# Sums of weight blocks: from the vector engine to accumulating DMAs of GpSimd's queue

## The chip, the cores and the metric

The kernel runs on one core of one Trainium2 chip. The metric is the device time of one execution in microseconds, and a lower time is better. Five engines have instruction queues of their own and work each through its own queue in order: TensorE (PE in the profile; PEld is its weight load), VectorE (DVE), ScalarE (ACT), GpSimd (POOL) and SyncE (SP). An instruction that waits holds up all that stands behind it on its engine.

## The reference

The reference is a trunk of two layers on 512 tokens of width 1024 in float32. Each layer mixes (attention, a short convolution and an RWKV recurrence side by side, with one input and one output projection), and then has an MLP, which is all that matters here:

```python
for l in range(DEPTH):                       # DEPTH = 2
    ...                                      # mixing, x = x + mixed @ w_out[l]
    h = rms_norm(x, norm_mlp_g[l])
    x = x + jnp.square(jax.nn.relu(h @ w_mlp_up[l])) @ w_mlp_down[l]
return rms_norm(x, final_norm_g)
```

`w_mlp_up` is 1024 x 4096 and `w_mlp_down` 4096 x 1024.

## The kernel before

Every float32 product is made of three passes of TensorE. A weight block (128 x 512 elements, 256 KB) is loaded, ScalarE casts it to a high part (`act.copy`), and a subtraction makes the low part; high by high, high by low and low by high are added up in PSUM. The moving operand is split the same way.

The up projection of a layer has 32 groups of 128 columns. The first eight (`up`) are done plainly. The other 24 go in 12 pairs per layer, 24 pairs in all: `two(i0, i1)` computes the groups `i0` and `i1` together by seven products instead of eight, a scheme of the Strassen-Winograd kind. Each group's weight is two blocks (`w11`, `w12` of `i0`; `w21`, `w22` of `i1`), and the sequence is cut in two halves of 256. The seven products, in TensorE's order, are p1 (`w11`), p5, p6, p2 (`w12`), p7, p3 and p4 (`w22`); p5, p6, p7 and p3 have sums of blocks as weights. One product is 12 matmuls of 128 x 256. The sums stand in tiles `s1` to `s4`, made by VectorE in `sum_` (line 1461). `both` (lines 1455 and 1456) splits a block or a sum: the cast on ScalarE writes `shi_…`, the subtraction on VectorE writes `slo_…`. This is done a pair ahead: the blocks of pair n+1 are split while pair n is multiplied. `blocks` makes the combinations of the moving operand, `th`, once per layer.

`square` takes the two outputs of a pair: VectorE applies relu and a scale (`r`, line 1400), ScalarE squares (`m`, line 1402), then `kept` splits the result into `mh` (ScalarE) and `ml` (GpSimd, line 1392). These are the moving operands of the down projection.

After nearly every pair comes `down(h, js)`: four `dn` tiles, each 12 matmuls of 128 x 512 into PSUM tag `mm`, which has two buffers. VectorE adds each tile to the residual `x` (line 1516), which frees its buffer. So a `dn` tile can't start before the tile two ahead of it has been added. The down weights come through `weights` (lines 339, 344 and 345: load by SyncE, cast `whi` by ScalarE, subtraction `wlo` by VectorE), in a ring of three sets and a fourth spare one: the cast for a tile of the next `down` is made when a `dn` tile of this one has freed a set. In layer 1, no `down` stands between the last two pairs; what is left goes to `last_group` at the end (`dnF`).

In the MLP the order of each engine's queue is set when the program is built, by a scheduler of the language's tile layer; in the mixing part it is written out by hand. A tile's semaphores follow from the program order of its readers and writers.

Of the kernel before, what the change touches and what calls it, by code (L numbers as in the profile page):

```python
# [10 lines left out]
F32 = mybir.dt.float32  # L11
F32R = mybir.dt.float32r
# [4 lines left out]
ALU = mybir.AluOpType  # L17
# [6 lines left out]
P = 128  # L24
# [244 lines left out]
def tile_trunk(ctx: ExitStack, tc: tile.TileContext, xT, wts, prm_d, cst_d, lora_d, gup_d, lam_d, fin_d, out):  # L269
    nc = tc.nc  # L270
    act, dve, pool = nc.scalar, nc.vector, nc.gpsimd
# [195 lines left out]
    def last_group(fp, wbase, mids):  # L467
# [21 lines left out]

        eps = cp.tile([P, 12], F32, tag="lsum", name="epsF")[:, :1]  # L490
        dve.memset(eps, EPS)
        eye = fp.tile([P, 4, P], F32R, tag="s1", name="eyeF")[:, 0]
        act.copy(eye, ident)

        def norm(half, sq):
            q = slice(half * H, (half + 1) * H)
            pt = psum("rp", 4, f"pssF{half}")
            for i, a in enumerate((acc[:, q], sq)):
                for b in range(2):

                    pe.matmul(pt[:, b:b + 1], a[:, b * P:(b + 1) * P], ones1, start=(i == 0 and b == 0), stop=True,
                              skip_group_check=True)
            yy, xt = [cp.tile([P, n], F32, tag=k, bufs=b, name=f"{k}F{half}") for k, b, n in (("rr", 2, NB), ("rsx", 3, 48))]
            yy, xx, t = yy[:, :2], xt[:, :2], xt[:, 24:26]
            hi, lo = [fp.tile([P, 4, P], F32R, tag=k, name=f"r{p}F{half}")[:, 0, :2] for p, k in (("hi", "s2"), ("lo", "s3"))]
            act.activation(t, pt[:, :2], AF.Sqrt, bias=eps, scale=1.0 / D)
            dve.tensor_scalar(xx, pt[:, :2], 1.0 / D, EPS, ALU.mult, ALU.add)
            dve.reciprocal(yy, t)
            act.copy(hi, yy)
            dve.tensor_tensor(t, yy, yy, ALU.mult)  # L510
            dve.scalar_tensor_tensor(t, t, -0.5, xx, ALU.mult, ALU.mult)
            dve.scalar_tensor_tensor(t, t, 1.5, yy, ALU.add, ALU.mult)
            dve.tensor_tensor(lo, t, hi.bitcast(F32), ALU.subtract)
            yield

            rb = [psum("rp", 4, f"prbF{half}_{i}") for i in range(1 + half)]
            for i, r in enumerate((hi, lo)):
                for p in rb:
                    for b in range(2):
                        pe.matmul(p[:, b * P:(b + 1) * P], r[:, b:b + 1].to_broadcast([P, P]), eye, start=(i == 0 and b == 0),  # L520
                                  stop=(i == 1), skip_group_check=True)
            rbs = fp.tile([P, H], F32, tag="c0", bufs=2, name=f"rbs{half}")
            act.copy(rbs, rb[-1][:, :H])
            os_ = []
            for j in range(NK):
                o = fp.tile([P, H], F32, tag=("p1", "p5", "u2", "c1")[j // 2], bufs=2, name=f"o{half}_{j}")
                if j in ((2, 5) if half else (2, 5, 6, 7)):
                    pool.tensor_tensor(o, x[j][:, q], rbs, ALU.mult)
                else:
# [39 lines left out]
    for l in range(L):  # L569
# [807 lines left out]
        with ExitStack() as mx:  # L1377
# [14 lines left out]
                pool.tensor_tensor(lo, m, hi.bitcast(F32), ALU.subtract)  # L1392
                mids.append((hi, lo))

            def square(cs, name):

                r = fp.tile([P, S], F32, tag="r", bufs=2, name=f"r{name}")
                for i, c in enumerate(cs):
                    q = slice(i * H, i * H + c.shape[1])
                    dve.scalar_tensor_tensor(r[:, q], c, 0.0, rs[:, q], ALU.max, ALU.mult)  # L1400
                m = fp.tile([P, S], F32, tag="m", bufs=3, name=f"m{name}")
                act.activation(m, r, AF.Square)
                kept(m)
# [25 lines left out]

            def blocks(k):  # L1430
                b1, b2 = bn[k], bn[k + 4]
                t = [fp.tile([P, 2, H], F32, tag=f"s{2 * (k % 2) + i + 1}", name=f"t{l}_{k}_{i}") for i in range(2)]
                dve.tensor_tensor(t[0][:, 0], b1[:, 1], b1[:, 0], ALU.subtract)
                dve.tensor_tensor(t[0][:, 1], b2[:, 1], t[0][:, 0], ALU.subtract)
                dve.tensor_tensor(t[1][:, 0], b2[:, 1], b1[:, 1], ALU.subtract)
                dve.tensor_tensor(t[1][:, 1], b2[:, 0], t[0][:, 1], ALU.subtract)
                hi, lo = th[k] = [fp.tile([P, 4, H], F32R, tag=f"t{p}{k}", name=f"t{p}{l}_{k}") for p in ("hi", "lo")]
                for i in range(2):
                    u = slice(2 * i, 2 * i + 2)
                    act.copy(hi[:, u], t[i])  # L1440
                    dve.tensor_tensor(lo[:, u], t[i], hi[:, u].bitcast(F32), ALU.subtract)

            def two(i0, i1):

                n = f"{l}_{i0}"
                wg = wbase + NG_IN + NG_OUT

                def raw(i, a):
                    t = fp.tile([P, 4, P], F32, tag="sraw", bufs=6, name=f"raw{n}_{i}_{a}")
                    nc.sync.dma_start(t.rearrange("p k c -> p (k c)"), wts[wg + i, :, a * P:(a + 4) * P])  # L1450
                    return t

                def both(src, name):
                    hi, lo = [fp.tile([P, 4, P], F32R, tag=f"s{p}", bufs=5, name=f"s{p}{n}_{name}") for p in ("hi", "lo")]
                    act.copy(hi, src)  # L1455
                    dve.tensor_tensor(lo, src, hi.bitcast(F32), ALU.subtract)  # L1456
                    return hi, lo

                def sum_(name, a, b, op):
                    t = fp.tile([P, 4, P], F32, tag=name, name=f"{name}{n}")  # L1460
                    dve.tensor_tensor(t, a, b, op)
                    return t

                def small(name):
                    return fp.tile([P, H], F32, tag=name, bufs=2, name=f"{name}{n}")

                def product(pt, w, moving, first=True):

                    whi, wlo = w
                    for k in range(4):  # L1470
                        ahi, alo = moving(k)
                        pe.matmul(pt, whi[:, k], ahi, start=(first and k == 0), stop=False, skip_group_check=True)
                        pe.matmul(pt, whi[:, k], alo, start=False, stop=False, skip_group_check=True)
                        pe.matmul(pt, wlo[:, k], ahi, start=False, stop=(k == 3), skip_group_check=True)

                blk = lambda d, q: lambda k: [p[:, q * H:(q + 1) * H] for p in acts[4 * d + k]]
                smm = lambda q: lambda k: [p[:, q] for p in th[k]]
                pa, pb = [psum("rp", 4, f"p{i}{n}")[:, :H] for i in "ab"]
                pc = psum("at", 2, f"pc{n}")[:, :H]
                c0 = fp.tile([P, S], F32, tag="c0", bufs=2, name=f"c0{n}")  # L1480
                w11 = raw(i0, 0)
                product(pa, both(w11, "p1"), blk(0, 0))
                p1 = small("p1")
                act.copy(p1, pa)
                w21 = raw(i1, 0)
                w22 = raw(i1, 4)
                s1 = sum_("s1", w21, w22, ALU.add)
                product(pb, both(s1, "p5"), smm(0))
                p5 = small("p5")
                dve.tensor_copy(p5, pb)  # L1490
                s2 = sum_("s2", s1, w11, ALU.subtract)
                product(pa, both(s2, "p6"), smm(1), False)
                u2 = small("u2")
                act.copy(u2, pa)
                w12 = raw(i0, 4)
                product(pc, both(w12, "p2"), blk(1, 0))
                dve.tensor_tensor(c0[:, :H], pc, p1, ALU.add)
                s3 = sum_("s3", w11, w21, ALU.subtract)
                product(pa, both(s3, "p7"), smm(2), False)
                c1 = small("c1")  # L1500
                act.copy(c1, pa)
                dve.tensor_tensor(c1, c1, p5, ALU.add)
                s4 = sum_("s4", w12, s2, ALU.subtract)
                product(pb, both(s4, "p3"), blk(1, 1), False)
                dve.tensor_tensor(c0[:, H:], pb, u2, ALU.add)
                square([c0], f"{n}_0")
                product(pa, both(w22, "p4"), smm(3), False)
                square([pa, c1], f"{n}_1")

            def down(h, js):  # L1510

# [96 lines left out]
```

## Time and profile before

| | us |
|---|---|
| runs, device time | 1241.35, 1242.42, 1243.07 |
| median | 1242.42 |
| profiled execution, span from first to last instruction | 1241.5 |
| TensorE busy | 1230.0 |
| VectorE busy | 912.1 |
| ScalarE busy | 675.0 |
| GpSimd busy | 368.0 |

The profiled execution is listed by its span; no device time of its own stands beside it, so the span is compared with the median of the runs, 0.9 us above it. The granted clock of TensorE is 0.998. The DMA queues moved 127.90 MB, 103 GB/s on average, nearly all of it on SyncE's queue. In the profile's rows, `out<-in` are the program's tile names without their numbers, `xN` is a count, and the brackets at the end of a row of the timeline give the idle time of the engine just before and what ended it. Rows "start us, us, engine line operation" come from the chain of waits or the timeline. MATMUL rows overlap each other, so their single durations don't add up to TensorE's time.

### The profile page before, as it was taken

To read this page: it belongs to the slowest core of one execution; us is meant where nothing else is said; L and a number is where in the kernel's file an instruction comes from. 1 tells how busy PE (TensorE), PEld (TensorE's weight loads), DVE (VectorE), ACT (ScalarE), POOL (GpSimd) and SP (SyncE) were. 2 spreads that over 40 slices of the span, in tenths; PEclk is the share of its full clock that TensorE was granted. 3 is DMA by queue.
4 is the path that set the end of the run, shared out by engine and by line. 5 is a ranking of instruction groups with operands and counts; after the bars stand their busy time and mean duration, and the time that the engine had idled before them with its cause. 6 is when DMAs were issued, how large, how long until landed. Compare 5 with 4: busy or idle time off the path is not lost.

```text
span 1241.5 us, 24974 instructions
## 1 busy us (share of the span) xinstructions
PE 1230.0 (99%) x9492; PEld 1055.0 (85%) x9492; DVE 912.1 (73%) x1776; ACT 675.0 (54%) x1410; POOL 368.0 (30%) x457
## 2 busy tenths in 40 slices
PE   9999999999999999999999999999999999999997
PEld 6888888888899998989887888888888999998987
DVE  6787888868767676765766777887687767676753
ACT  6785655548445454544464657464583445454542
POOL 1263637342311111111026355464231211111111
PEclk9999999999999999999999999999999999999999
DMA  6523324142433333321235244332433333333121
GB/s 216 163 87 99 105 96 111 53 153 85 136 102 98 107 94 106 99 85 44 69 106 164 79 118 119 89 83 73 158 102 120 102 102 98 107 94 107 55 68 68
DMA packets 84695, 127.90 MB, mean 103 GB/s; under 512 B 21472, under 2 KB 25568, under 8 KB 84576
## 3 DMA queue, kind: packets, MB, share of 16 engines
q1 hardware_dynamic: 83568, 125.64, 33.1%
q8 instruction: 74, 1.21, 0.4%
q10 hardware_dynamic: 1008, 0.68, 0.2%
q14 instruction: 45, 0.37, 0.1%
HBM read 117.11 MB, written 9.18 MB: 102 GB/s over the span
## 4 chain that ended last, share of the span: by engine, by line
PE 93%; ACT 2%; DVE 2%; DMA 1%; POOL 1%; issue 1%; ACTq 0%; POOLq 0%; DVEq 0%
PE dn L282 25%; PE pj L282 20%; PE pa L282 11%; PE po L282 8%; PE up L282 7%; PE pb L282 6%; PE dnF L282 4%; PE pc L282 3%; PE sc L282 1%; DMA raw<-wts 1%; PE ptt L287 1%; PE pg L282 1%; PE pyy L282 1%; PE pzw L282 1%; PE pst L282 1%
## 5 line engine op out<-in xcount | busy, mean ns | idle before, releaser
L1392 POOL TENSOR_TENSOR ml<-m,mh 128x512 fp32r<-128x512 f32 x64 | 108.9, 1716 | 481.0 <-ACT mh L1391 340.6
L344 ACT CAST whi<-raw 128x512 fp32r<-128x512 f32 x142 | 87.4, 619 | 162.4 <-PE dn L282 152.8
L282 PE MATMUL dn<-mh,whi 128*128 128x512 f32 x448 | 174.8, 390 | 0.1
L282 PE MATMUL dn<-ml,whi 128*128 128x512 f32 x448 | 174.6, 390 | 0.0
L282 PE MATMUL dn<-mh,wlo 128*128 128x512 f32 x448 | 174.5, 390 | 0.0
L683 POOL TENSOR_TENSOR wlo<-raw,whi 128x512 fp32r<-128x512 f32 x84 | 111.0, 1321 | 213.1 <-ACT whi L671 175.4
L282 PE MATMUL pj<-ahim,whi 128*128 128x512 f32 x392 | 156.7, 400 | 0.4 <-DVE vf L1278 0.4
L282 PE MATMUL pj<-ahim,wlo 128*128 128x512 f32 x392 | 156.4, 399 | 0.0
L282 PE MATMUL pj<-alom,whi 128*128 128x512 f32 x392 | 155.9, 398 | 0.0
L1516 DVE TENSOR_TENSOR x<-dn,x 128x512 f32<-128x512 f32 x112 | 77.3, 690 | 103.1 <-PE dn L282 103.1
L671 ACT CAST whi<-raw 128x512 fp32r<-128x512 f32 x142 | 87.6, 617 | 83.3 <-PE pj L282 25.1
L345 DVE TENSOR_TENSOR wlo<-raw,whi 128x512 fp32r<-128x512 f32 x142 | 115.0, 811 | 11.2 <-ACT whi L344 8.3
L282 PEld LDWEIGHTS dn<-mh,wlo 128*128 128x128 f32 x448 | 84.1, 188 | 17.8
L282 PEld LDWEIGHTS dn<-mh,whi 128*128 128x128 f32 x448 | 84.1, 188 | 17.5 <-issue 0.4
L282 PEld LDWEIGHTS dn<-ml,whi 128*128 128x128 f32 x448 | 84.1, 188 | 16.7
L1455 ACT CAST shi_p<-s 128x512 fp32r<-128x512 f32 x96 | 59.6, 621 | 70.1 <-PE pa L282 55.1
L282 PEld LDWEIGHTS pj<-ahim,whi 128*128 128x128 f32 x392 | 73.9, 188 | 14.1 <-issue 0.8
L282 PEld LDWEIGHTS pj<-alom,whi 128*128 128x128 f32 x392 | 73.9, 188 | 13.9 <-issue 0.5
L282 PEld LDWEIGHTS pj<-ahim,wlo 128*128 128x128 f32 x392 | 73.9, 188 | 13.8 <-issue 0.2
L1456 DVE TENSOR_TENSOR slo_p<-s,shi_p 128x512 fp32r<-128x512 f32 x96 | 67.9, 708 | 19.7 <-ACT shi_p L1455 17.2
L282 PE MATMUL pa<-tlo,shi_p 128*128 128x256 f32 x288 | 81.3, 282 | 0.0
L282 PE MATMUL pa<-thi,shi_p 128*128 128x256 f32 x288 | 81.2, 282 | 0.0
(414 smaller groups left out, 3208.1 us busy)
## 6 DMA issues: line engine op xcount, KB each, us to landing
raw<-wts SPq DMA_DIRECT2D x389, 256.0 KB, 2.7
qs<-dqhi SPq DMA_DIRECT2D x24, 128.0 KB, 3.7
ks<-dkhi SPq DMA_DIRECT2D x24, 128.0 KB, 3.7
x<-xT SPq DMA_DIRECT2D x8, 256.0 KB, 4.6
dqhi<-qhi SPq DMA_DIRECT2D x6, 256.0 KB, 3.4
dqlo<-qlo SPq DMA_DIRECT2D x6, 256.0 KB, 3.4
dkhi<-khi SPq DMA_DIRECT2D x6, 256.0 KB, 2.7
dklo<-klo SPq DMA_DIRECT2D x6, 256.0 KB, 3.5
```

Source lines behind the costliest of these rows:

```text
L282: ins = nc.tensor.matmul(*a, **k)
L287: ins = nc.tensor.transpose(*a, **k)
L344: act.copy(hi[:, :n], raw[:, :n])
L345: (pool if a and lean[0] else dve).tensor_tensor(lo[:, :n], raw[:, :n], hi[:, :n].bitcast(F32), ALU.subtract)
L671: yield act.copy(hi[:, k0:k1], raw[:, k0:k1])
L683: yield eng.tensor_tensor(lo[:, k0:k1], raw[:, k0:k1], hi[:, k0:k1].bitcast(F32), ALU.subtract)
L1392: pool.tensor_tensor(lo, m, hi.bitcast(F32), ALU.subtract)
L1455: act.copy(hi, src)
L1456: dve.tensor_tensor(lo, src, hi.bitcast(F32), ALU.subtract)
L1516: dve.tensor_tensor(x[j], pt, x[j], ALU.add)
```

## The change

`sum_` goes. `begun` has SyncE load the first block of a sum straight into the sum's tile, and `plus` adds a further block to it by a DMA of GpSimd's queue with `accum_op=ALU.add`. Such a transfer can only add. So a pair's second output is computed with its sign turned: then every block enters with a plus, `square` takes the minimum with zero in place of the maximum before it squares, and `blocks` turns signs to match. The sums for p5, p6 and p3 are now one running sum in one tile (`w21`, then `+ w22`, `+ w11`, `+ w12`), and p7's is a second one (`w11 + w21`). Each tag has two buffers. A further block can only be added when both halves of the split have read the sum before it. Per pair: four sums of VectorE are gone, four accumulating DMAs of GpSimd are new, and nine blocks are loaded instead of four. The last group's small tiles take the same tags.

```diff
-                t = [fp.tile([P, 2, H], F32, tag=f"s{2 * (k % 2) + i + 1}", name=f"t{l}_{k}_{i}") for i in range(2)]
-                dve.tensor_tensor(t[0][:, 0], b1[:, 1], b1[:, 0], ALU.subtract)
-                dve.tensor_tensor(t[0][:, 1], b2[:, 1], t[0][:, 0], ALU.subtract)
+                t = [fp.tile([P, 2, H], F32, tag=("s1", "s3")[i], bufs=2, name=f"t{l}_{k}_{i}") for i in range(2)]
+                dve.tensor_tensor(t[0][:, 0], b1[:, 0], b1[:, 1], ALU.subtract)
+                dve.scalar_tensor_tensor(t[0][:, 1], t[0][:, 0], -1.0, b2[:, 1], ALU.mult, ALU.subtract)
                 dve.tensor_tensor(t[1][:, 0], b2[:, 1], b1[:, 1], ALU.subtract)
-                dve.tensor_tensor(t[1][:, 1], b2[:, 0], t[0][:, 1], ALU.subtract)
+                dve.scalar_tensor_tensor(t[1][:, 1], t[0][:, 1], -1.0, b2[:, 0], ALU.mult, ALU.subtract)
...
-                def sum_(name, a, b, op):
-                    t = fp.tile([P, 4, P], F32, tag=name, name=f"{name}{n}")
-                    dve.tensor_tensor(t, a, b, op)
+                def begun(tag, i, a):
+                    t = fp.tile([P, 4, P], F32, tag=tag, bufs=2, name=f"{tag}{n}")
+                    nc.sync.dma_start(t.rearrange("p k c -> p (k c)"), wts[wg + i, :, a * P:(a + 4) * P])
+                    return t
+                def plus(t, i, a):
+                    pool.dma_start(t.rearrange("p k c -> p (k c)"), wts[wg + i, :, a * P:(a + 4) * P], accum_op=ALU.add)
                     return t
...
-                w21 = raw(i1, 0)
                 w22 = raw(i1, 4)
-                s1 = sum_("s1", w21, w22, ALU.add)
-                product(pb, both(s1, "p5"), smm(0))
+                sm = plus(begun("s1", i1, 0), i1, 4)
+                product(pb, both(sm, "p5"), smm(0))
...
-                s2 = sum_("s2", s1, w11, ALU.subtract)
-                product(pa, both(s2, "p6"), smm(1), False)
+                product(pa, both(plus(sm, i0, 0), "p6"), smm(1), False)
...
-                s3 = sum_("s3", w11, w21, ALU.subtract)
-                product(pa, both(s3, "p7"), smm(2), False)
+                product(pa, both(plus(begun("s3", i0, 0), i1, 0), "p7"), smm(2), False)
...
-                s4 = sum_("s4", w12, s2, ALU.subtract)
-                product(pb, both(s4, "p3"), blk(1, 1), False)
+                product(pb, both(plus(sm, i0, 4), "p3"), blk(1, 1), False)
...
-                square([pa, c1], f"{n}_1")
+                square([pa, c1], f"{n}_1", ALU.min)
```

TensorE's order is the same in both programs. That of the other engines is not. ScalarE's queue in layer 0 while pair `0_10` is multiplied, before; `shi0_11_…` are the casts for the next pair, `m0_10_…` and `mh0_…` the outputs of this one, `whi78_0` the first weight of the next `down`:

```order
L1455 CAST shi0_11_p5_5377<-s10_11_5375 128x512
L1455 CAST shi0_11_p6_5397<-s20_11_5395 128x512
L1501 COPY c10_10_5212<-pa0_10_5107 128x256
L1455 CAST shi0_11_p2_5417<-raw0_11_11_4_5415 128x512
L1455 CAST shi0_11_p7_5436<-s30_11_5434 128x512
L1402 ACTIVATE m0_10_0_5236<-r0_10_0_5234 128x512
L1391 CAST mh0_12_5238<-m0_10_0_5236 128x512
L1402 ACTIVATE m0_10_1_5261<-r0_10_1_5258 128x512
L344 CAST whi78_0_5510<-raw78_0_5508 128x512
L1391 CAST mh0_13_5263<-m0_10_1_5261 128x512
```

The same place after the change:

```order
L1455 CAST shi0_11_p5_5370<-s10_11_5367 128x512
L1504 COPY c10_10_5207<-pa0_10_5103 128x256
L1455 CAST shi0_11_p6_5389<-s10_11_5367 128x512
L1402 ACTIVATE m0_10_0_5230<-r0_10_0_5228 128x512
L1402 ACTIVATE m0_10_1_5255<-r0_10_1_5252 128x512
L1391 CAST mh0_12_5232<-m0_10_0_5230 128x512
L1391 CAST mh0_13_5257<-m0_10_1_5255 128x512
L1455 CAST shi0_11_p2_5409<-raw0_11_11_4_5407 128x512
L1455 CAST shi0_11_p7_5429<-s30_11_5426 128x512
L344 CAST whi78_0_5502<-raw78_0_5500 128x512
```

The cast for p6 reads the tile that p5's cast read (`s10_11`), and both `m`, both `mh` and the casts for p2 and p7 now stand between it and the `down` weight.

VectorE's queue at the same place, before; `x0` and `x1` are the additions of the first and second `dn` tile:

```order
L1456 TENSOR_TENSOR slo0_11_p7_5437<-s30_11_5434,shi0_11_p7_5436 128x512
L1461 TENSOR_TENSOR s30_12_5674<-raw0_12_12_0_5591,raw0_12_24_0_5611 128x512
L1516 TENSOR_TENSOR x0_69<-dn0_2_0_5267,x0_69 128x512
L345 TENSOR_TENSOR wlo78_0_5511<-raw78_0_5508,whi78_0_5510 128x512
L1516 TENSOR_TENSOR x1_70<-dn0_2_1_5287,x1_70 128x512
```

And after the change:

```order
L1456 TENSOR_TENSOR slo0_11_p6_5390<-s10_11_5367,shi0_11_p6_5389 128x512
L1518 TENSOR_TENSOR x0_69<-dn0_2_0_5261,x0_69 128x512
L1456 TENSOR_TENSOR slo0_11_p2_5410<-raw0_11_11_4_5407,shi0_11_p2_5409 128x512
L1456 TENSOR_TENSOR slo0_11_p7_5430<-s30_11_5426,shi0_11_p7_5429 128x512
L345 TENSOR_TENSOR wlo78_0_5503<-raw78_0_5500,whi78_0_5502 128x512
L1518 TENSOR_TENSOR x1_70<-dn0_2_1_5281,x1_70 128x512
```

The subtractions for p6, p2 and p7 of the next pair stand among the additions of this pair's `dn` tiles now; before, they were all ahead of them.

GpSimd's queue at the same place, after the change (before, there are only the `ml`):

```order
L1392 TENSOR_TENSOR ml0_11_5020<-m0_9_1_5017,mh0_11_5019 128x512
L1467 DMA s30_12_5664<-wts 128x512
L1467 DMA s10_12_5605<-wts 128x512
L1467 DMA s10_11_5367<-wts 128x512 x2
L1392 TENSOR_TENSOR ml0_12_5233<-m0_10_0_5230,mh0_12_5232 128x512
L1392 TENSOR_TENSOR ml0_13_5258<-m0_10_1_5255,mh0_13_5257 128x512
```

Between the `ml` of two pairs stand four accumulations: the sum for p7 and the first one for p5, both of the pair after next, and then the second and the third of the next pair's running sum.

More of the change, by code (lines that the diff above doesn't have):

```diff
@@ L491, in last_group @@
         dve.memset(eps, EPS)
-        eye = fp.tile([P, 4, P], F32R, tag="s1", name="eyeF")[:, 0]
+        eye = fp.tile([P, 4, P], F32R, tag="s1", bufs=2, name="eyeF")[:, 0]
         act.copy(eye, ident)
@@ L504, in norm @@
             yy, xx, t = yy[:, :2], xt[:, :2], xt[:, 24:26]
-            hi, lo = [fp.tile([P, 4, P], F32R, tag=k, name=f"r{p}F{half}")[:, 0, :2] for p, k in (("hi", "s2"), ("lo", "s3"))]
+            hi, lo = [fp.tile([P, 4, P], F32R, tag="s3", bufs=2, name=f"r{p}F{half}")[:, 0, :2] for p in ("hi", "lo")]
             act.activation(t, pt[:, :2], AF.Sqrt, bias=eps, scale=1.0 / D)
@@ L1393, in kept, with square @@
                 mids.append((hi, lo))
-            def square(cs, name):
+            def square(cs, name, side=ALU.max):
                 r = fp.tile([P, S], F32, tag="r", bufs=2, name=f"r{name}")
@@ L1399, in square @@
                     q = slice(i * H, i * H + c.shape[1])
-                    dve.scalar_tensor_tensor(r[:, q], c, 0.0, rs[:, q], ALU.max, ALU.mult)
+                    dve.scalar_tensor_tensor(r[:, q], c, 0.0, rs[:, q], side, ALU.mult)
                 m = fp.tile([P, S], F32, tag="m", bufs=3, name=f"m{name}")
```

## The prediction

> **What bounds the kernel now.** I read the page's busy times and its chain of waits first, then the busy times by stage, what TensorE waited for, and one pair of the MLP in order of time. The times of engines and the shares of the chain that ended last:
>
> ```profile
> PE 1230.0 (99%) x9492; PEld 1055.0 (85%) x9492; DVE 912.1 (73%) x1776; ACT 675.0 (54%) x1410; POOL 368.0 (30%) x457
> PE 93%; ACT 2%; DVE 2%; DMA 1%; POOL 1%; issue 1%; ACTq 0%; POOLq 0%; DVEq 0%
> ```
>
> TensorE is busy for 1230.0 of 1241.5 us. The change lies in the pairs alone, so two stretches that hold pairs only (us, then busy us of each engine, granted clock, DMA share, GB/s):
>
> ```profile
> 348.00:588.00 240.00, 240.00 (x1534) 218.79 (x1533) 173.62 (x293) 111.20 (x205) 36.02 (x22) 1.00 0.30 92
> 956.00:1176.00 220.00, 220.00 (x1409) 200.68 (x1408) 161.98 (x273) 103.88 (x191) 33.47 (x20) 1.00 0.31 96
> ```
>
> There TensorE has no idle time at all. The list of what TensorE waited for (us in total, times, longest) has eight rows, from the first to the last here, and none has a line of the pairs:
>
> ```profile
> PE idle L282 <- DVE zero L394: 1.2, 1, 1.2
> ...
> PE py L282 <- ACT rt L1178: 0.4, 1, 0.4
> ```
>
> One period, a pair's seven products and four `dn` tiles, by the chain of waits (start, us):
>
> ```profile
> 399.08 10.93 PE dn L282 x48
> 420.01 10.93 PE dn L282 x48
> ```
>
> 420.01 - 399.08 = 20.93 us. The order keeps TensorE's instructions as they are, so a period can only grow, by what makes TensorE wait.
>
> **What is removed.** The sums on VectorE:
>
> ```profile
> L1461 DVE TENSOR_TENSOR s<-raw,raw x48: 674/693/1781, 313.3 to 1157.5; 128x512 f32<-128x512 f32 x48
> L1461 DVE TENSOR_TENSOR s<-s,raw x24: 674/684/687, 315.6 to 1154.0; 128x512 f32<-128x512 f32 x24
> L1461 DVE TENSOR_TENSOR s<-raw,s x24: 676/692/693, 320.4 to 1169.0; 128x512 f32<-128x512 f32 x24
> ```
>
> 96 by 0.69 us are 66 us of VectorE's 912. They lie beside a full TensorE, so their removal is worth 0.
>
> **What is added: a chain through transfers.** VectorE now subtracts the high part of the sum for p5, GpSimd then issues the accumulation of `w11` into the same tile, and only when that has landed can ScalarE cast the sum for p6. Call L the time of one accumulation from issue to landing. On ScalarE's queue the p6 cast now stands ahead of m, m, mh, mh, p2, p7 and the next `dn` weight's cast, and VectorE's subtraction for that weight ahead of the eviction of the second `dn` tile. The present times of these instructions (start, us):
>
> ```profile
> 394.72 0.62 ACT L1455 CAST shi_p<-s 128x512 fp32r<-128x512 f32 x1 [0.53 <-PE pc L282]
> 400.74 0.62 ACT L1391 CAST mh<-m 128x512 fp32r<-128x512 f32 x1
> 401.27 0.62 ACT L1402 ACTIVATE m<-r 128x512 f32<-128x512 f32 x1
> 401.80 0.61 ACT L344 CAST whi<-raw 128x512 fp32r<-128x512 f32 x1
> 395.37 0.69 DVE L1456 TENSOR_TENSOR slo_p<-s,shi_p 128x512 fp32r<-128x512 f32 x1
> 402.50 1.19 DVE L345 TENSOR_TENSOR wlo<-raw,whi 128x512 fp32r<-128x512 f32 x1
> 404.60 0.69 DVE L1516 TENSOR_TENSOR x<-dn,x 128x512 f32<-128x512 f32 x1 [0.91 <-PE dn L282]
> 405.21 0.68 DVE L345 TENSOR_TENSOR wlo<-raw,whi 128x512 fp32r<-128x512 f32 x1
> 407.12 0.39 PE L282 MATMUL dn<-mh,whi 128*128 128x512 f32 x1
> ```
>
> The subtraction for p5 ends at 395.37 + 0.69 = 396.1, so the sum for p6 has landed at 396.1 + L. Eight ScalarE instructions follow; back to back they start 0.53 apart (400.74, 401.27, 401.80), so the last ends at 396.1 + L + 7 x 0.53 + 0.61 = 400.4 + L. The weight's subtraction adds 0.61 (404.60 to 405.21 is how close two of them start), the eviction 0.69: 401.7 + L. Its PSUM tag has two buffers, so the fourth `dn` tile, which starts at 407.12, needs this eviction: slack 407.1 - 401.7 = 5.4, call it 5.3 with the hops between engines. The eviction of the first tile, now right behind p6's subtraction, is due one tile earlier (10.93 / 4 = 2.7 us) but has seven of these instructions fewer ahead of it, so the second decides.
>
> A second delay, d, comes off that slack. GpSimd's subtractions (`ml`) and VectorE's fall on each other, and one of the two is then late:
>
> ```profile
> 401.50 3.35 POOL L1392 TENSOR_TENSOR ml<-m,mh 128x512 fp32r<-128x512 f32 x2 [17.61 <-PE dn L282]
> 940.47 1.29 POOL L1392 TENSOR_TENSOR ml<-m,mh 128x512 fp32r<-128x512 f32 x1 [2.60 <-ACT mh L1391]
> 1179.95 1.42 DVE L1456 TENSOR_TENSOR slo_p<-s,shi_p 128x512 fp32r<-128x512 f32 x1 [0.37 <-ACT shi_p L1455]
> L1456 DVE TENSOR_TENSOR slo_p<-s,shi_p x96: 676/692/1776, 316.2 to 1179.9; 128x512 fp32r<-128x512 f32 x96
> ```
>
> Two `ml` take 3.35 beside VectorE and 1.29 each alone; VectorE's took 1.19 and 1.42 instead of 0.69, once 1.776. So d is 0.5 (1.19 - 0.69) to 1.1 (1.776 - 0.692), and the slack 4.2 to 4.8. I take 4.4, since two or three subtractions of VectorE now stand beside the two `ml`. Without any d only the last pair would lose at the L below, some 2 us, and nothing in the others.
>
> **How long is L?** No accumulating transfer is in this trace. The nearest rows, KB each and us from issue to landing, and GpSimd's shortest instruction of the arithmetic kind:
>
> ```profile
> raw<-wts SPq DMA_DIRECT2D x389, 256.0 KB, 2.7
> x<-xT SPq DMA_DIRECT2D x8, 256.0 KB, 4.6
> dn<-nd SPq DMA_DIRECT2D x6, 64.0 KB, 2.2
> 897.23 1.02 POOL L369 TENSOR_TENSOR rrf<-rsx,ones 128x4 f32<-128x4 f32 x1
> L1392 POOL TENSOR_TENSOR ml<-m,mh 128x512 fp32r<-128x512 f32 x64 | 108.9, 1716 | 481.0 <-ACT mh L1391 340.6
> ```
>
> Lower end: 2.7, a plain load of the same size. Added to it: the old content has to be read too, a third stream of 256 KB, at (2.7 - 2.2) per 192 KB 0.7 us; GpSimd has to do something to issue it, taken as its shortest instruction, 1.0; and more company, below, 0.4. Together 4.8, which I take; an estimate. It lies nearer to the lower end because the load rows of the pairs' own line are the 2.7. Upper end: 4.6 (the loads of the crowded start) + 0.7 + 1.7 (a full instruction of GpSimd) = 7.0. A negative end is excluded: TensorE waits for nothing there.
>
> A variant of it: GpSimd can't issue while VectorE works. VectorE is busy for 173.62 of 240 us in the pairs, so an issue would find it busy 0.72 of the time and wait for half of 0.69 us: L longer by 0.25 on average, and by 0.69 at worst, +6 to +16 us more, 1260 to 1270, inside the forecast's own range below. The Trainium skill's page "SBUF — State Buffer", section "Who interferes with whom", has such a rule: it says that a transfer issued by GpSimd can be held up by VectorE where the two share a port, though not by a plain `tensor_tensor`, which it only infers; by it the 4.8 would stand. Only the 1.42 against 0.69 above, the two engines' own instructions, is shown here.
>
> **Traffic.** Per pair nine 256-KB blocks instead of four, with four `dn` weights: 13 instead of 8. The share of 0.30 becomes 0.30 x 13/8 = 0.49, about 150 GB/s; the crowded start of the kernel ran at 216 (the first of 40 slices):
>
> ```profile
> GB/s 216 163 87 99 105 96 111 53 153 85 136 102 98 107 94 106 99 85 44 69 106 164 79 118 119 89 83 73 158 102 120 102 102 98 107 94 107 55 68 68
> ```
>
> So the rate is no bound. The part of L that is transfer (2.7 - 0.7 = 2.0) grows by about 2.0 x 0.19 = 0.4. SyncE now issues the first block of each sum, one row more per pair, and that issue waits for the readers of the pair two back. Behind it stand weight loads, issued far ahead:
>
> ```profile
> 387.71 3.05 SPq L339 DMA_DIRECT2D raw<-wts  x2
> ```
>
> These are there at 390.8 and cast at 401.80: 11 us of cover, so 0. GpSimd's `ml` now stand behind accumulations; their `dn` is about one period later (they ended at 404.85, the next `dn` starts at 420.01), 15 us of cover, so 0. The third accumulation (p3) is issued at 397.4 + L and lands at 397.4 + 2L; its product is the last but one ahead of the `dn` at 420.01, so at 420.01 - 2 x 1.43 = 417.1 (the row of two products is below), and a cast and a subtraction (1.3) precede it: 0 up to L of about 9.
>
> **Edits that cost nothing.** `min` for `max`, and a scalar form for a plain difference: 0.42 us both.
>
> ```profile
> 397.43 0.42 DVE L1502 TENSOR_TENSOR c<-c,p 128x256 f32<-128x256 f32 x1
> 399.91 0.42 DVE L1400 SCALAR_TENSOR_TENSOR r<-pa,rsf 128x256 f32<-128x256 f32 x1
> ```
>
> The tags of the last group change the place of tiles only, with TensorE ahead of them by whole groups.
>
> **The last pair.** In layer 1 no `dn` stands between the last two pairs, so the cover of 10.93 is gone.
>
> ```profile
> 1172.56 0.69 DVE L1456 TENSOR_TENSOR slo_p<-s,shi_p 128x512 fp32r<-128x512 f32 x1
> 1174.84 2.85 PE pa L282 x24
> ```
>
> The second accumulation is issued at 1173.25, p6 is ready at 1173.25 + L + 0.62 + 0.69, the third lands L after that, and p3 is ready 1.3 later: 1175.9 + 2L. TensorE wants p3 five products of 1.44 after the pair's start at 1176.1: 1183.3. Loss 2L - 7.4, and with 0.75 of d twice 2L - 5.9: 3.7 us at 4.8.
>
> **The sum.** A period loses L - 4.4 in 21 pairs (eleven in layer 0 and ten in layer 1 have a next pair and a `dn` between): 21 x 0.4 = 8.4. With 3.7 for the last: +12.1. The profiled span is 1241.5 and the median of the three runs 1242.4, 0.9 (0.07%) over it, so 1254.5.
>
> **Where the order shows it.** The rows on ScalarE, VectorE and GpSimd that stand ahead of the prediction carry these terms: the p6 cast before the two m, and the four accumulations between one pair's `ml` and the next's.
>
> **Rivals.** (1) Hidden: L is under the slack of about 4.2. For it: 2.7 + 1.0 = 3.7 if the third stream runs beside the others. Then 0 in the pairs and at most 2 x 4.2 - 5.9 = 2.5 at the end: 1242.4 to 1245. It decides at L = 4.2; not slower. The page "DMA: Bandwidth & Descriptors" of the Trainium skill, section "Anatomy of one DMA — SWDGE (gpsimd) path", has some 2.0 us fixed plus bytes at 436 GB/s for a transfer of GpSimd: 2.6 us for 256 KB, an estimate, and it speaks of plain ones; by it the time would be 1242.4. No run here shows it yet.
> (2) Long: L is 5.6 to 7, 21 x 1.6 + 6.1 = +40 at L = 6, 1282, and 21 x 2.6 + 8.1 = +63 at 7, 1305. Kin to it: GpSimd is held until each accumulation lands. Four and two `ml` then take 4L + 3.35 of a period, over 20.93 from L = 4.4; at 4.8 it is 1.6 x 24 = +39, 1281, at 5.6 +115, 1358. For it speaks that accumulations on one tile have to be in order; against it that DMA issues of the other queues run side by side in the trace (two in 3.05).
> (3) Faster: VectorE has 66 us less to do. Only a wait for VectorE could pay it, and the eight rows of TensorE's waits hold none in the pairs: 1239 at best.
>
> **How the numbers follow.** A measurement of this kernel tells about 0.2% (2.5 us) from no change. Forecast (L from 4.4 to 5.6, 1245 to 1273) 0.40; hidden 0.33; long or held 0.24; faster 0.03. Faster 0.03, same 0.33, slower 0.64. The range goes from 1241, the hidden case at the fastest run, to 1305, the upper end of L; beyond lies about half of the held case, and the faster one. The forecast's own range is 1245 to 1273.
>
> **What would show it.** L in the list of DMA issues of GpSimd's queue; 96 of them; VectorE's busy time down by 66; TensorE's waits naming the `dn` tiles, L - 4.4 before the fourth, and a period of 20.93 + that; ScalarE idle before the p6 cast on a DMA. Wrong would be: L under 4.2, a slack other than 4.4, or GpSimd's queue late by itself.

## The result, and the profile after

The changed kernel takes 1324.62 us in the median of four runs (1321.27 to 1327.35), against 1242.74 (1241.35 to 1243.42) before: 1.0656 times as long, 95% interval 1.0638 to 1.0674. The prediction was 1254.5 us in a range of 1241 to 1305; the direction was right and the size was not. In the profiled execution the span grew from 1241.5 to 1321.5 us, by 80.0.

The busy times, and the shares of the chain that ended last:

```profile
PE 1253.1 (95%) x9492; PEld 1062.7 (80%) x9492; DVE 884.8 (67%) x1680; ACT 665.7 (50%) x1410; POOL 431.0 (33%) x553
PE 61%; DMA 14%; DVE 8%; issue 8%; ACT 7%; POOL 2%; ACTq 0%; POOLq 0%; DVEq 0%; SPq 0%
```

TensorE does the same 9492 matmuls and is on only 61% of the chain, where it was on 93%. VectorE has 27 us less to do rather than 66, since some of its instructions got longer: 22 subtractions take 2.2 to 2.5 us instead of 0.69. The two stretches at the same times (busy us, granted clock, DMA share, GB/s); the second one now begins 45 us ahead of the first product of layer 1's pairs:

```profile
348.00:588.00 240.00, 216.84 (x1333) 192.38 (x1331) 145.22 (x220) 95.36 (x182) 60.26 (x59) 0.99 0.59 139
956.00:1176.00 220.00, 201.60 (x1138) 174.81 (x1138) 130.80 (x197) 85.56 (x162) 53.82 (x53) 0.95 0.60 147
```

Where TensorE was busy throughout, a tenth of the time is idle, and the clock is under 1.00. The longest item of what TensorE waited for (us in total, times, longest us) has a name:

```profile
PE dn L282 <- DVE x L1518: 48.2, 24, 2.6
```

This is the wait for the eviction two `dn` tiles back. One period by the chain of waits, with some short pieces left out (start, us, what):

```profile
494.68 3.04 PE dn L282 x12
497.72 1.31 PE pa L282 x11
...
500.43 2.96 DMA s<-wts
...
504.06 0.89 POOL s L1467
504.95 0.16 issue
505.11 5.21 DMA s<-wts
...
510.39 0.04 ACT shi_p L1455
...
513.66 0.03 DVE slo_p L1456
...
516.09 0.68 DVE slo_p L1456
516.77 0.60 DVE wlo L345
517.37 0.61 DVE x L1518
517.98 0.04 issue
518.02 2.11 PE dn L282 x8
```

The load at 500.43 and the issue at 504.06 belong to the sum for p5 of the pair after next; the accumulation that p6 needs is issued behind them at 505.11. What it waits for is p5's subtraction, which ends 0.41 us before; this distance is 0.40 to 0.41 in all 21 pairs, with another issue just ahead or none:

```profile
504.01 0.69 DVE L1456 TENSOR_TENSOR slo_p<-s,shi_p 128x512 fp32r<-128x512 f32 x1
```

The reader sees the forecast chain, link by link: an accumulation from 505.11 to 510.32, p6's cast, a stretch until 516.09 in which VectorE gets nothing done, the weight's subtraction, the eviction, and then the fourth `dn` tile at 518.02. The next fourth tile is 23.34 us after the one of 494.68, not 20.93. The transfers themselves, in the list of DMA issues (KB each, median us to landing):

```profile
raw<-wts SPq DMA_DIRECT2D x365, 256.0 KB, 3.0
s<-wts POOLq DMA_DIRECT2D x96, 256.0 KB, 4.6
s<-wts SPq DMA_DIRECT2D x48, 256.0 KB, 3.0
```

I split the 80 us by the starts of the `dn` groups in the two profiles. Up to the second group of a layer, 6.3 us are lost in layer 0 and 8.0 in layer 1. The periods from there to the end of the pairs lose 30.8 in layer 0 and 30.1 in layer 1, 2.8 and 3.3 each (11 and 9 periods). Between the layers 1.0 comes back. The last 5.6 are 2.0 at the fourth tile of the last of these groups, the 21st of its kind, and 3.7 in the last pair, which has no `dn` ahead of it. That is 79.8.

### The profile page after: what moved, and what is told of

Read it like the earlier page. It is cut to its first block, busy times and chain, and to the rows that moved or that the text cites. A ratio compares the mean times of both kernels' runs of the same rounds, so it can differ in the third digit from the quotient of the medians.

```text
span 1321.5 us, 25228 instructions
## 1 busy us (share of the span) xinstructions
PE 1253.1 (95%) x9492; PEld 1062.7 (80%) x9492; DVE 884.8 (67%) x1680; ACT 665.7 (50%) x1410; POOL 431.0 (33%) x553
## 3 DMA queue, kind: packets, MB, share of 16 engines
q0 software_dynamic: 13824, 25.17, 12.2%
## 4 chain that ended last, share of the span: by engine, by line
PE 61%; DMA 14%; DVE 8%; issue 8%; ACT 7%; POOL 2%; ACTq 0%; POOLq 0%; DVEq 0%; SPq 0%
PE pj L282 19%; DMA s<-wts 13%; PE dn L282 12%; PE po L282 8%; PE pa L282 5%; PE dnF L282 3%; DVE slo_p L1456 2%; ACT shi_p L1455 2%; ACT m L1402 2%; PE pb L282 2%; DVE wlo L345 2%; PE pc L282 1%; PE up L282 1%; PE sc L282 1%; DVE x L1518 1%
## 5 line engine op out<-in xcount | busy, mean ns | idle before, releaser
L282 PE MATMUL dn<-mh,whi 128*128 128x512 f32 x448 | 182.1, 406 | 51.3 <-DVE x L1518 48.2
L1467 POOL DMA_DIRECT2D s<-wts x96 | 85.2, 907 | 439.5 <-DVE c L1501 139.7
L282 PE MATMUL dn<-mh,wlo 128*128 128x512 f32 x448 | 179.1, 400 | 1.0 <-DVE wlo L345 1.0
L282 PE MATMUL dn<-ml,whi 128*128 128x512 f32 x448 | 178.9, 399 | 0.0
L1456 DVE TENSOR_TENSOR slo_p<-raw,shi_p 128x512 fp32r<-128x512 f32 x72 | 89.8, 1247 | 48.7 <-ACT shi_p L1455 41.8
L1392 POOL TENSOR_TENSOR ml<-m,mh 128x512 fp32r<-128x512 f32 x64 | 94.7, 1608 | 60.2 <-ACT mh L1391 60.2
L345 DVE TENSOR_TENSOR wlo<-raw,whi 128x512 fp32r<-128x512 f32 x142 | 104.0, 733 | 14.3 <-ACT whi L344 12.3
```

The costliest lines, as they stand in the source:

```text
L282: ins = nc.tensor.matmul(*a, **k)
L345: (pool if a and lean[0] else dve).tensor_tensor(lo[:, :n], raw[:, :n], hi[:, :n].bitcast(F32), ALU.subtract)
L1467: pool.dma_start(t.rearrange("p k c -> p (k c)"), wts[wg + i, :, a * P:(a + 4) * P], accum_op=ALU.add)
```

## The experiments

Theory A: each pair loses what the second accumulation's landing, with the queue behind it, runs over the slack of the fourth `dn` tile. Rival B: the accumulating transfers cost by themselves, by GpSimd's issues, collisions or traffic. Three smaller questions came with it: VectorE's standstill (C), the clock after a wait (D and E), the starts of the layers (F). All times stand against runs of the kernel before on the same chip, 1242.2 to 1242.5 us.

**The algebra alone.** The sums stay on VectorE; signs, `min` and `blocks` are those of the change.

```diff
-                sm = plus(begun("s1", i1, 0), i1, 4)
+                w21 = raw(i1, 0)
+                sm = sum_("s1", w21, w22)        # VectorE, ALU.add; s2, s3, s4 likewise
```

> The kernel before with the second output's sign turned (sums with plus only, scalar_tensor_tensor in blocks, min in square), all sums still by VectorE. Theory A: the algebra costs nothing, 1241.5 to 1243.5. Rival: the scalar forms or the order that follows cost something, 1245 or more.

1242.53 us, ratio 1.0000 (0.9991 to 1.0009). The sign costs nothing.

**The same transfers, not accumulating.**

```diff
-                    pool.dma_start(t..., wts[wg + i, :, a * P:(a + 4) * P], accum_op=ALU.add)
+                    pool.dma_start(t..., wts[wg + i, :, a * P:(a + 4) * P])
```

> The changed kernel with the 96 transfers of GpSimd's queue made plain: same blocks, same tiles, same waits, same order on every engine, but each overwrites the tile and adds nothing (so the sums are left out and the output is not the reference's). Theory A (each pair loses what the second transfer's landing, and the queue behind it, runs over the slack of the fourth dn tile): the second accumulation took 5.2 us from issue to landing in the changed kernel; a plain one should take 0.9 of issue and 2 to 2.7 of transfer, about 3.6. Then the wait of 2.1 to 2.6 us before the fourth dn tile falls to 0.5 to 1.0, the slow tiles after it become rare, and the time is 1255 to 1275. Rival B (it is GpSimd's issuing, its collisions with VectorE or the traffic, and not how long an accumulation takes): the waits stay, 1315 to 1330.

1262.46 us, ratio 1.0153 (1.0137 to 1.0170): 62 of the 82 us go with one argument. GpSimd's DMA queue in the changed kernel, and then its queue and transfers here (packets, MB, share of 16 engines' span; KB, us to landing):

```profile
q0 software_dynamic: 13824, 25.17, 12.2%
```

```profile
q0 software_dynamic: 7680, 25.17, 6.0%
s<-wts POOLq DMA_DIRECT2D x96, 256.0 KB, 3.3
```

The issues on GpSimd by the tile view, changed kernel first (ns min/median/max):

```profile
L1467 POOL DMA_DIRECT2D s<-wts x96: 857/877/1507, 312.6 to 1256.0; - x96
```

```profile
L1467 POOL DMA_DIRECT2D s<-wts x96: 536/546/747, 312.7 to 1198.3; - x96
```

And TensorE's wait here, 11.0 us where it was 48.2:

```profile
PE dn L282 <- DVE x L1518: 11.0, 9, 2.0
```

For the same bytes, accumulation takes nearly twice the packets, twice the time of the DMA engines, 0.33 us more of GpSimd per issue, and 1.3 us more to land in the median. From the end of p5's subtraction to the start of p6's cast the changed kernel took 4.6 to 7.5 us over 21 pairs, 5.85 in the mean; this one took 3.3 to 5.8, 4.20 in the mean, and periods in which it took 3.7 or less have the old 20.93. A smaller part of the 62 us is not the transfer's: the path from p6's cast to the end of the second eviction is 7.1 us here and was 7.55. Rival B, as far as it concerns the number of issues and the bytes that are loaded, falls.

**Half of the elements.**

```diff
-                    pool.dma_start(t..., wts[wg + i, :, a * P:(a + 4) * P], accum_op=ALU.add)
+                    pool.dma_start(t[:, :2]..., wts[wg + i, :, a * P:(a + 2) * P], accum_op=ALU.add)
```

> The changed kernel with each accumulation of half the elements (the first 256 of 512, 128 KB; the other half of each sum is left out). From p5's subtraction to p6's cast the changed kernel takes 5.4 to 7.5 us, 5.9 in the mean, and plain transfers of full size 3.6 where nothing collides. If what accumulation adds goes with the bytes, half of the 2.0 to 2.3 goes and some transfer with it: 4.4 to 4.8; if it is fixed, 5.3 or more. The order on ScalarE and VectorE differs a little here (p2's cast ahead of the second m). With 4.6 the wait before the fourth dn tile would be about 1 us, 20 us less in all, and few slow tiles after it: 1280 to 1300 against 1310 to 1324.

1283.46 us, ratio 1.0332 (1.0316 to 1.0348).

```profile
q0 software_dynamic: 13824, 12.59, 7.0%
s<-wts POOLq DMA_DIRECT2D x96, 128.0 KB, 3.5
```

The same interval is 4.11 us in the mean and 3.6 to 3.8 in the undisturbed pairs, shorter than expected: half of an accumulation lands as soon as a whole plain transfer. The packets are as many as before, and the time of the DMA engines falls from 12.2% to 7.0%. So most of what accumulation adds goes with the bytes; a plain transfer of 128 KB was not run beside it. The kernel is slower than the plain version although the transfers take as long: in this version's order the subtractions for p2 and p7 stand ahead of the first eviction on VectorE, the third `dn` tile waits for that one, and an undisturbed period takes 21.5 us.

Not every accumulation of the changed kernel takes as long as the second one. The third of each pair, issued when no other is under way, lands after 4.1 us in the mean (3.9 to 4.6 over 21 pairs). The second lands after 5.4 (4.1 to 7.0); in all pairs but the last of layer 0 it is issued about 1.0 us behind the first accumulation of the pair after next. In that last pair, with nothing ahead of it, it took 4.1, and the period 22.3 us where all others took 23.2 or more. With plain transfers the third takes 2.9 and the second 3.7. So some 1.3 us of the second one look like waiting for its neighbour. An estimate from the share fits this: 12.2% of 1321.5 us over 96 transfers is 1.7 us of all 16 DMA engines each, and the two are issued 1.0 us apart. No run takes the neighbour away by itself, so this part is not shown by an experiment.

**VectorE's standstill.** The timeline of the changed kernel beside two `ml` of GpSimd:

```profile
512.72 2.89 POOL L1392 TENSOR_TENSOR ml<-m,mh 128x512 fp32r<-128x512 f32 x2
513.66 2.51 DVE L1456 TENSOR_TENSOR slo_p<-raw,shi_p 128x512 fp32r<-128x512 f32 x1 [1.32 <-ACT shi_p L1455]
516.09 0.68 DVE L1456 TENSOR_TENSOR slo_p<-s,shi_p 128x512 fp32r<-128x512 f32 x1
```

One subtraction takes 2.51 us instead of 0.69. I let GpSimd fill the tile instead of reading two others, with nothing moved on VectorE, ScalarE or TensorE:

```diff
-                pool.tensor_tensor(lo, m, hi.bitcast(F32), ALU.subtract)
+                pool.memset(lo.bitcast(F32), 0.0)
```

> The changed kernel with GpSimd's ml subtraction replaced by a fill with zeros of the same tile: GpSimd still writes 128x512 in the same place of the chain, but reads nothing (the low part of the MLP's middle values is left out, so the output is not the reference's). VectorE's, ScalarE's and TensorE's order is that of the changed kernel. Theory A with VectorE's standstill beside the two ml as its second half (2.1 us of the wait): the wait of 2.1 to 2.6 before the fourth dn tile falls to 0.3 to 0.6, and with it most of the slow dn tiles after it (0.8 per pair): 1265 to 1285. Rival C (only the transfer counts): no change, 1318 to 1330.

1272.68 us, ratio 1.0245 (1.0221 to 1.0268). p2's subtraction in the same place of the timeline, and TensorE's wait:

```profile
518.80 0.69 DVE L1456 TENSOR_TENSOR slo_p<-raw,shi_p 128x512 fp32r<-128x512 f32 x1 [1.31 <-ACT shi_p L1455]
```

```profile
PE dn L282 <- DVE x L1518: 12.4, 22, 0.8
```

From p6's cast to the end of the second eviction, all 21 pairs of the changed kernel take 7.54 to 7.58 us and those of this one 5.75 to 5.76. So the standstill is 1.8 us of the path, 38 us in 21 pairs. With it went some 9 us at the starts of the layers and all six slow tiles told of below; against that p6's cast came 0.2 us later behind p5's subtraction here. In all, 52 of the 82 us hang on it, since it lies on a path already over its slack. The Trainium skill's page "SBUF — State Buffer", section "Who interferes with whom", says that VectorE with two SBUF inputs contends with a GpSimd instruction that reads SBUF and not with one that only writes it; 2.51 against 0.69 agrees.

The other way round, `ml` made by VectorE:

```diff
-                pool.tensor_tensor(lo, m, hi.bitcast(F32), ALU.subtract)
+                dve.tensor_tensor(lo, m, hi.bitcast(F32), ALU.subtract)
```

> The changed kernel with the ml subtraction made by VectorE instead of GpSimd. In the changed kernel VectorE stood still for 2.4 us beside two ml of GpSimd (512.72 to 515.61) with p2's subtraction, the dn weight's and the eviction of the second dn tile behind it. Theory A with this delay as its second half: 2.4 us go and two subtractions of 0.61 come, so 1.2 us less wait per pair, 21 x 1.2 = 25, and some of the slow dn tiles with it: 1285 to 1300. Rival C (VectorE's standstill is no part of it, only the transfer counts): the two subtractions are added to the wait, 1324 + 25 = about 1350, or 1324 if they fall behind the eviction.

1303.57 us, ratio 1.0496 (1.0464 to 1.0528), 21 us less than the changed kernel and a little above what I expected. A new wait stands behind it. Both `ml` now precede the first eviction on VectorE, and the third `dn` tile waits for that one:

```profile
411.62 1.29 DVE L1392 TENSOR_TENSOR ml<-m,mh 128x512 fp32r<-128x512 f32 x2 [0.87 <-ACT mh L1391]
412.83 0.68 DVE L1518 TENSOR_TENSOR x<-dn,x 128x512 f32<-128x512 f32 x1
413.57 0.50 PE L282 MATMUL dn<-mh,whi 128*128 128x512 f32 x1 [1.24 <-DVE x L1518]
```

**The accumulation taken out of the path, with more traffic.** p6's sum is begun anew in its own tile, so that it can be issued a pair ahead:

```diff
-                product(pa, both(plus(sm, i0, 0), "p6"), smm(1), False)
+                s2 = plus(plus(begun("s2", i1, 0), i1, 4), i0, 0)
+                product(pa, both(s2, "p6"), smm(1), False)
...
-                product(pb, both(plus(sm, i0, 4), "p3"), blk(1, 1), False)
+                product(pb, both(plus(s2, i0, 4), "p3"), blk(1, 1), False)
```

> The changed kernel with the sum for p6 begun anew in a tile of its own (w21, + w22, + w11) instead of in p5's, so that no accumulation that p6 needs waits for a subtraction; 11 blocks and 5 accumulations per pair instead of 9 and 4, loads in a ring of 5 instead of 6, one tile instead of two for p7's sum. Theory A: the wait before the fourth dn tile goes, the starts of the layers may still lose some 4 to 8 us each: 1243 to 1262. Rival B (traffic, or GpSimd's issues and their collisions): more of each, 1324 or more.

1262.41 us, ratio 1.0162 (1.0147 to 1.0177). The two stretches at the same times, and TensorE's longest wait:

```profile
348.00:588.00 240.00, 239.72 (x1503) 217.02 (x1502) 164.54 (x249) 109.70 (x203) 72.18 (x72) 1.00 0.71 170
956.00:1176.00 220.00, 219.12 (x1355) 196.76 (x1354) 152.15 (x230) 99.76 (x184) 65.70 (x66) 0.99 0.75 183
```

```profile
PE dn L282 <- ACT whi L344: 7.4, 2, 4.8
```

With five accumulations a pair rather than four, and 170 to 183 GB/s rather than 139 to 147, TensorE is all but full in the pairs. Neither traffic nor accumulations as such are the loss in the pairs. By the `dn` groups, 17 of the 20 us left are at the two starts (8.0 in layer 0, 9.1 in layer 1).

**Only the sums that can be issued a pair ahead.** `w11` and `w12` are added by VectorE, in place.

```diff
-                product(pa, both(plus(sm, i0, 0), "p6"), smm(1), False)
+                dve.tensor_tensor(sm, sm, w11, ALU.add)
+                product(pa, both(sm, "p6"), smm(1), False)
...
-                product(pb, both(plus(sm, i0, 4), "p3"), blk(1, 1), False)
+                dve.tensor_tensor(sm, sm, w12, ALU.add)
+                product(pb, both(sm, "p3"), blk(1, 1), False)
```

> The changed kernel with only the sums for p5 and p7 made by accumulating transfers (one each, issued a pair ahead); w11 and w12 are added into the running sum by VectorE, in place. Theory A: no transfer stands between p5's subtraction and p6's cast, so 1243 to 1260 (what is left is the starts of the layers). Rival B (each accumulating transfer costs by itself): half of the 82 us remain, about 1283.

1249.65 us, ratio 1.0057 (1.0042 to 1.0072), every period 20.93.

**The third block too.** As the version just shown, but `w12` comes by an accumulation again.

> p5's and p7's first sums and the third block (w12, for p3) by accumulating transfers, w11 added by VectorE in place: a serial accumulation stays in each pair, but it is the one that the prediction gave cover up to 9 us. Theory A: the periods stay at 20.93, and against the version without it (1249.7) only the last pair, whose cover is gone, loses 0 to 3 us: 1248 to 1254. Rival (any accumulation that waits for a subtraction holds GpSimd's queue and with it the ml and the next sums): 1 us or more a pair, 1270 or more.

1248.19 us, ratio 1.0050 (1.0036 to 1.0063), every period 20.93. An accumulation that waits for a subtraction costs nothing where something else covers it. This version has three of the change's four accumulations a pair; what it lacks is the second one, and with that the scheduler put p2's and p7's casts ahead of the `m`.

**The starts of the layers.** All sums of the first pair of each layer are made by VectorE:

```diff
                 def plus(t, i, a, w=None):
+                    if i0 == N_ONE:
+                        dve.tensor_tensor(t, t, w, ALU.add)
+                        return t
                     pool.dma_start(...)
```

In the changed kernel:

> The changed kernel with the sums of the first pair of each layer made by VectorE, all other pairs as changed. By the start of dn groups, the changed kernel loses 6.3 us up to the second dn group of layer 0 and 8.0 in layer 1, since nothing is issued ahead there. Theory A: these 14 us go, but the second pair's accumulations are still issued late: 1308 to 1318. Rival F (the starts are late for another reason, such as loads that queue up): under 3 us, 1321 to 1327.

1311.94 us, ratio 1.0557 (1.0524 to 1.0589): 12.7 us less. The same edit in the version with only p5's and p7's sums by transfers:

> The version with only the sums for p5 and p7 by accumulating transfers (1249.7 in its run), with all sums of the first pair of each layer made by VectorE too. Theory A: its 7 us were starts, 1.3 in layer 0, and about 4 in layer 1: 1242.5 to 1246, the time of the kernel before or 0.2% over it, not under it, since TensorE has nothing left to wait for in either. Rival: the accumulating transfers cost something in every pair: 1248 to 1251.

1243.18 us, ratio 1.0006 (0.9996 to 1.0016): no difference from the kernel before, with 44 sums off VectorE. No version is faster than the kernel before.

**The clock.** After a wait, the fourth `dn` tile of the changed kernel sometimes ran slowly, in six of 21 pairs. The first three matmuls of one such tile, and the window around it (granted clock 0.64):

```profile
397.16 0.75 PE L282 MATMUL dn<-mh,whi 128*128 128x512 f32 x1 [2.14 <-DVE x L1518]
397.70 0.63 PE L282 MATMUL dn<-ml,whi 128*128 128x512 f32 x1
398.13 0.63 PE L282 MATMUL dn<-mh,wlo 128*128 128x512 f32 x1
```

```profile
397.10:401.80 4.70, 4.64 (x14) 3.73 (x15) 1.80 (x4) 0.22 (x1) 0.89 (x1) 0.64 0.81 247
```

Matmuls start 0.43 us apart there, and 0.23 elsewhere. I put matmuls on zeros into the gap.

```diff
+                    if j % 4 == 3 and 0 < h < 2 * N_KG - 1:
+                        idle = psum("at", 2, f"warm{l}_{h}_{j}")
+                        for _ in range(9):
+                            pe.matmul(idle, wz[:, :P], wz, start=True, stop=True)
                     pt = psum("mm", 2, f"dn{l}_{h}_{j}")
```

> The changed kernel with nine matmuls on zeros (bf16, 128x512, into a PSUM buffer that nobody reads) put ahead of each fourth dn tile that follows a pair, so that TensorE works where it waited; 22 x 9 matmuls of about 0.22 us, 2 us each time. Theory D (the fourth dn tile runs at half speed for part of its time because TensorE's granted clock falls after an idle time of about 2 us; this is 0.8 us a pair, about 17 us of the 82): the tile is back at 2.73 us, the granted clock at 1.00, and the kernel gets faster by work that is added: 1304 to 1314. Rival E (the slow tiles come from their operands or from the DMA traffic that starts there, 247 GB/s): the clock stays, and the added matmuls cost up to 10 us where they are longer than the wait: 1324 to 1336.

1322.13 us, ratio 1.0629 (1.0599 to 1.0660), which can't be told from the changed kernel's. The same window:

```profile
397.10:401.80 4.70, 4.70 (x26) 3.52 (x24) 3.37 (x7) 0.62 (x1) 0.81 (x1) 1.00 0.87 257
```

The clock is back at 1.00 under more DMA traffic (0.87, 257 GB/s), and no fourth tile is slow any more. So the idle time lowers the clock, and rival E falls. How long the wait is doesn't decide it alone: the waits ahead of the six slow tiles were 1.8 to 2.6 us, and after two others of 2.6 us the tile ran at full speed. My expected 17 us was too much: the six slow tiles are each 1.0 to 1.6 us too long, about 9 us. Some of that was taken by the added matmuls, where they outlast the wait, and the transfers took longer in layer 1 (6.2 us from subtraction to cast, against 5.8). Why they did stays open. The Trainium skill's page "TensorE: Matmul & The Clock Gate", section "Part 1: The HAM clock gate", has an idle TensorE's clock at half rate; 0.43 against 0.23 agrees. It gives an idle window of some 3.4 us as the condition; here 1.8 to 2.6 us were enough in six cases, so the measurement decides.

## Why the prediction was wrong

**Where the loss is: right.** That TensorE bounds the kernel, that VectorE's 96 sums are worth nothing, that the second accumulation stands ahead of the `dn` weight's cast and so of the second eviction, and that the fourth `dn` tile pays: each link is in the chain shown above, and periods are back at 20.93 where that accumulation is made plain and takes 3.7 us or less with the order unchanged, and where it is taken out of the path (the scheduler's order then changes with it).

**The size of L: too small.** The step took 4.8 us from issue to landing, and the mean of the 21 is 5.4. Another 0.5 lies around it (0.41 ahead of the issue, 0.07 behind the landing), for which the sum had 0.1 of hops in all. So 5.85 us pass where 4.8 were put down. The transfer by itself was not the part that was too small: 2.7 + 0.7 + 1.0 = 4.4 against 4.1 for the third accumulation, which has no neighbour. Too small was the company, put at 0.4: with the first accumulation of the pair after next just ahead of it in the same queue, the second one takes 1.3 us more than the third. That the neighbour is the reason rests on these rows and the one pair without it, as told above. The upper end of 7.0 held every one of the 21.

**The delay d: too small.** The step took 0.9 of 0.5 to 1.1 and measured 1.8. Its rows were of one subtraction that met one `ml`; in the new order both `ml` come as one block just ahead of p2's subtraction, which then waits for both. Without `ml` reads, the path from cast to eviction is 5.76; the prediction had 11.06 from p5's subtraction to the fourth tile (396.06 to 407.12) and a slack of 5.3, which is the same 5.76.

These two, 1.05 and 0.9, make 2.0 us a pair: a loss of 0.4 was forecast and 2.4 came. Over 21 pairs that is 50 us of 63 (the 61 of the 20 periods and the 2.0 at the last group's fourth tile). Of the rest, 9 are the slow tiles, and 3 come because a tile took 0.15 us longer after a wait at full clock too (2.64 us from its first matmul to its last, 2.49 without a wait). Both terms sat at a threshold, where 2.0 us of error in a sum of 11.5 is a factor of six in what is left over it. The range varied L and kept d and the slack, so it ended at 1305.

**Missing: the starts.** The sum had no term for the first pair of a layer, 14.3 us of the 80. There p5's cast waits for the first accumulations, which the prediction had in mind as issued a pair ahead. Start and duration of p5's cast in layer 0, after and before:

```profile
319.99 0.62 ACT L1455 CAST shi_p<-s 128x512 fp32r<-128x512 f32 x1 [6.47 <-DMA s<-wts]
```

```profile
314.04 0.62 ACT L1455 CAST shi_p<-s 128x512 fp32r<-128x512 f32 x1 [0.37 <-DVE s L1461]
```

**Missing: the clock.** About 9 us by the slow tiles of the pairs and 1.6 by one at the start of layer 1, none of which can be seen where TensorE never waits.

**The last pair: the number right, the path wrong.** 3.7 were forecast and 3.7 measured, but by luck. The prediction has TensorE wait for p3's sum, behind two accumulations. It didn't wait there. It waited 1.95 us ahead of p6, for ScalarE's copy of p1 (line 1490), which empties the PSUM tile that p6 needs and stands on ScalarE's queue behind the late p6 cast, both `m` and both `mh`:

```profile
1257.23 0.45 PE L282 MATMUL pa<-thi,shi_p 128*128 128x256 f32 x1 [1.95 <-ACT p L1490]
1258.00:1260.00 2.00, 2.00 (x11) 2.00 (x11) 2.00 (x2) 0.22 (x1) 1.37 (x2) 0.50 0.60 103
```

The rest came at a granted clock of 0.50 behind that wait. The third accumulation is on time here.

**The rivals.** "Hidden" failed with L. "Long" (1282 at L = 6) had about the 5.85 us, and lacked the larger d, the starts and the clock. "Held" is not seen: GpSimd issues the next transfer 1.05 us after the last (504.06, 505.11), without waiting for its landing. "Faster" found nothing to pay it, as argued. The terms set to 0 held: traffic (139 to 147 GB/s against the 150 estimated; 183 with 2 us lost in the pairs), the third accumulation, the sign. The Trainium skill's page "DMA: Bandwidth & Descriptors", section "Anatomy of one DMA — SWDGE (gpsimd) path", gives 2.6 us for a transfer of GpSimd of this size, an estimate from its figures; 3.3 was measured for plain ones and 4.6 for accumulating ones, so for these the measurement decides.

## What to carry to other kernels

Work moved off an engine that has time to spare gains nothing, and a transfer put between two steps of a chain brings its whole latency to every in-order queue behind it; look for the instruction queued behind the waiting one, not for the one that waits. Where a sum of delays ends near its slack, vary every term in the range, not only the unknown one, and price the first and the last round apart, since nothing is issued ahead there. An accumulating transfer was free here where it could be issued a round ahead, or where another stretch covered it. Look at what stands just ahead of a transfer in its queue, too.

## What the runs showed of the hardware

An accumulating transfer of GpSimd's queue cost twice the DMA engines' time of a plain one for the same bytes (12.2% against 6.0%). It took 4.1 us against 2.9 to land 256 KB when no other was under way, and 5.4 against 3.7 about 1 us behind another one; 128 KB landed about as fast as 256 KB plain (3.5 and 3.3 in the median). Its issue took GpSimd 0.88 us against 0.55. A VectorE subtraction stood still for both of GpSimd's, 2.51 us instead of 0.69, and not beside a fill. And waits of 1.8 to 2.6 us were enough, in six of 21 cases, for a `dn` tile at about half speed.
